# Running the recurrence's chunks of two head pairs kind by kind, with its gram products in quarters of the matmul array

## The chip, the cores and the metric

One core of one Trainium2 chip runs the whole program. The metric is device time in microseconds (us) of that core, the median of three runs. In the rows PE is the matmul engine (TensorE) and PEld its weight loads, DVE is VectorE, ACT is ScalarE, POOL is GpSimd, SP is the engine that issues most of the transfers, and L1612 is line 1612 of the kernel.

## What is computed

Two transformer blocks follow each other on 512 tokens of width 1024, all in float32. The first one has a gated linear recurrence, a convolution module, cross attention and feed-forward layers. The second one, in which the change lies, adds two mixers, a bidirectional RWKV-7 recurrence and a neighbourhood attention, and then a mixture of 32 experts. What matters here is the recurrence, with 8 heads of 64 channels and two directions d:

```python
def rwkv_step(S, inp):
    r_t, w_t, k_t, v_t, kk_t, a_t = inp
    sa = jnp.einsum('dbhij,dbhj->dbhi', S, -kk_t)
    S = (S * w_t[..., None, :] + sa[..., :, None] * (kk_t * a_t)[..., None, :]
         + v_t[..., :, None] * k_t[..., None, :])
    y = jnp.einsum('dbhij,dbhj->dbhi', S, r_t)
    return S, y
...
    S0 = jnp.zeros((2, B, RWKV_HEADS, HEAD_DIM, HEAD_DIM), jnp.float32)
    _, ys = lax.scan(rwkv_step, S0, xs)
    y_f = ys[:, 0].transpose(1, 0, 2, 3)
    y_b = jnp.flip(ys[:, 1].transpose(1, 0, 2, 3), axis=1)
    y = y_f + y_b
```

## The kernel before, in words

The kernel does not step token by token. It cuts the 512 tokens into 8 chunks of 64, and inside a chunk the steps become matrix products; only the 64x64 state passes from chunk to chunk. The 8 heads form 4 pairs p. One call `chunk(p, c)` does chunk c of both heads e of a pair and of both directions d: head 0 has partitions 0 to 63, head 1 has 64 to 127. There are 32 calls, with p running fastest.

What one call does, kind by kind, with the lines of the kernel before:

- L1577 and L1579 (in `fetch`, two calls ahead): two transfers of 64 KB (`w2`) and one of 192 KB (`bkv`), issued on SP. Each has three buffers.
- L1606: two transposes of the keys, copied by ACT to `bt` (L1607).
- L1612: the gram products, four matmuls of 64 rows by 128 columns. Each head has its own accumulator. A whole 128x128 product is made, of which one row half is masked into `w2` (L1615, DVE, 64x256) and a quarter into `rb` (L1617, DVE, 64x128). So DVE has four mask operations in each call.
- L1622: POOL scales the state by the decay into `ss`.
- L1626: four matmuls of the state with `w2` into `rh`, copied by DVE (L1629).
- L1633: four matmuls with the solved system `gt` into two accumulators, one for each head, copied into `su` by DVE and ACT (L1637).
- L1643: four matmuls for the state's update, with four DVE operations L1647 that write the next `su`.
- L1654 and L1658: eight matmuls for the output, added up in one accumulator `py` of both heads and added to the result by ACT or DVE (L1662 to L1666).

Each float32 matmul of these lines shows as two records in the trace. There are 5 accumulators of the kind `acc` and 3 of the kind `aux`.

Other work is put between the calls, as filler. It is the dense products (L524, L525, L526: three matmuls 128x512 for one block of a product in two-part float32), the neighbourhood attention (L1320 scores, L1350 transposes, L1357 values, and L635 and L1306), and the gates. Two strings of digits, `GATE` and `REST`, say how many steps of filler are released after each of the 32 calls. Within that, a scheduler sets the order of each engine's instructions when the program is built, so the code's order is not the engine's order: matmuls of neighbouring calls and of the filler are mixed, and each engine then runs its own list in order. After the last chunk of a head pair `finish` (L1676 onward) makes its normalised output.

Of the kernel before, what the change touches and what calls it, by code (L numbers as in the profile page):

```python
# [2 lines left out]

# [5 lines left out]
F32 = mybir.dt.float32  # L9
# [7 lines left out]
P = 128  # L17
S = 512
# [14 lines left out]
AHD = 2  # L33
# [178 lines left out]
HALF = (slice(0, 64), slice(64, P))  # L212
# [232 lines left out]
class Kernel:  # L445
# [689 lines left out]
    def final_norm(self):  # L1135


        nc = self.nc
        gf = self.v("final_norm", 0, DT)
        gg = self.C.tile([P, DT], F32, name="gg")  # L1140
        nc.vector.tensor_mul(gg, gf, self.v("norm1_g_2", 0, DT))
        xs = [self.split(t, scale=gg[:, i:i + 1]) for i, t in enumerate(self.x)]
        among = self.aheads(xs, "w_in_2", 0, range(8), (12, 13, 4, 0))
        for _ in range(6):
            next(among)
        r = self.rsqrt(self.by_token(*self.total(self.x, True, ends=ENDS)), 4, 1.0 / D)
# [10 lines left out]
        rb = self.M.tile([P, S], F32, name="rb", bufs=2)  # L1157
        nc.vector.tensor_copy(rb, self.spread(rr))
        rx = self.M.tile([P, S], F32, name="rb", bufs=2)
# [412 lines left out]

    def fetch(self, p, c):

        w2 = self.R.tile([P, 2, 2, P], F32, name="w2", bufs=AHD + 1)
        for e, a in enumerate(HALF):
            self.nc.sync.dma_start(w2[a, e], self.rec[p][c, a])  # L1577
        bkv = self.R.tile([P, 3, P], F32, name="bkv", bufs=AHD + 1)
        self.nc.sync.dma_start(bkv, self.bkv[p][c])  # L1579
        return w2, bkv  # L1580

    def chunk(self, p, c, w2, bkv):

        nc = self.nc
        R, M = self.R, self.M
# [2 lines left out]
        gt = self.gt[p // 2][:, n:n + 9:8]  # L1588


        own = lambda: R.tile([P, 2, 2, 2, 64], F32, name="su", bufs=5)
        if c == 0:
            self.su[p] = own()
            for e, a in enumerate(HALF):
# [7 lines left out]
        rb = R.tile([P, 2, 64], F32, name="rb", bufs=3)  # L1602
        bt = R.tile([P, 2, 2, 64], F32, name="bt", bufs=3)
        ps = self.acc()
        for d in range(2):
            nc.tensor.transpose(ps[:, d * P:(d + 1) * P], bk[:, d], self.idn)  # L1606
        nc.scalar.copy(bt.rearrange("p d e j -> p (d e j)"), ps[:, :2 * P])  # L1607
        for e in range(2):
            a, b = HALF[e], HALF[1 - e]
            ps = self.acc()  # L1610
            for d in range(2):
                nc.tensor.matmul(ps[:, d * P:(d + 1) * P], bk[a, d], w2[a, e, d], start=True,  # L1612
                                 stop=True)
            g = ps[:, :2 * P].rearrange("p (d t) -> p d t", d=2)
            nc.vector.tensor_mul(w2[b, e], g[b],  # L1615
                                 self.c("mk")[b, None, :].to_broadcast([64, 2, P]))
            nc.vector.tensor_mul(rb[a], g[a, :, 64:],  # L1617
                                 self.c("mi")[a, None, :].to_broadcast([64, 2, 64]))
        if c < 7:
            q = M.tile([P, 2, 64], F32, name="ss", bufs=4)  # L1620
            for e, a in enumerate(HALF):
                {'v': nc.vector, 'g': nc.gpsimd}[EB].tensor_mul(q[a], su[a, 0, e], el[a, :, c:c + 1].to_broadcast([64, 2, 64]))  # L1622
        pr = self.aux()
        for d in range(2):
            for e, a in enumerate(HALF):
# [1 line left out]
                                 start=True, stop=True)  # L1627
        rh = R.tile([P, 2, 64], F32, name="rh", bufs=2)
        nc.vector.tensor_copy(rh.rearrange("p d i -> p (d i)"), pr[:, :P])  # L1629
        pu = [self.aux(), self.aux()]  # L1630
        for d in range(2):
            for e, a in enumerate(HALF):
                nc.tensor.matmul(pu[e][a, d * 64:(d + 1) * 64], gt[a, d], rh[a, d],  # L1633
                                 start=True, stop=True)
        for e, a in enumerate(HALF):
            f = {'v': nc.vector.tensor_copy, 's': nc.scalar.copy}[EU[e]]
            f(su[a, 1, e].rearrange("p d i -> p (d i)"), pu[e][a, :P])  # L1637
        if c < 7:
            new = self.su[p] = own()
            pss = self.aux()  # L1640
            for d in range(2):
                for e, a in enumerate(HALF):
                    nc.tensor.matmul(pss[a, d * 64:(d + 1) * 64], bt[:, d, e], su[:, 1, e, d],  # L1643
                                     start=True, stop=True)
            for d in range(2):
                for e, a in enumerate(HALF):
                    nc.vector.scalar_tensor_tensor(new[a, 0, e, d], pss[a, d * 64:(d + 1) * 64],  # L1647
                                                   el[a, d, c:c + 1], q[a, d], op0=ALU.mult,
                                                   op1=ALU.add)
        py = self.aux()  # L1650

        for d in range(2):
            for e, a in enumerate(HALF):
                nc.tensor.matmul(py[a, d * 64:(d + 1) * 64], su[:, 0, e, d], w2[:, e, d, 64:],  # L1654
                                 start=d == 0, stop=False)
        for d in range(2):
            for e, a in enumerate(HALF):
                nc.tensor.matmul(py[a, d * 64:(d + 1) * 64], su[a, 1, e, d], rb[a, d], start=False,  # L1658
# [35 lines left out]
    def second_mixer(self):  # L1694
# [3 lines left out]
        with self.tc.tile_pool(name="systems", bufs=1) as G, \  # L1698
# [19 lines left out]
            self.Y, self.ya = self.x[:4], {}  # L1718
            with self.tc.tile_pool(name="chunks", bufs=1) as self.R:
                other, out = chain(near, gates), self.near_out()  # L1720
                gl = self.get("gl", self.R.tile([P, S], F32, name="gl"))
                ends = []
                slots = [(p, c) for c in range(8) for p in range(4)]
                recs = {n: self.fetch(*slots[n]) for n in range(AHD)}
                for n, (p, c) in enumerate(slots):
                    if n + AHD < len(slots):
                        recs[n + AHD] = self.fetch(*slots[n + AHD])
                    self.chunk(p, c, *recs.pop(n))
                    for g, at in ((gates, GATE), (other, REST)):
                        for _ in range(int(at[n])):  # L1730
                            next(g, None)
                    if c == 7:
                        if p == 0:
                            for _ in other:
                                pass
                        ends.append(self.finish(p, gl))
                        next(ends[p])
                        next(out)
                        if p > 1:
                            next(ends[p - 2])  # L1740
                            next(out)
                for e in ends[2:]:
                    next(e)
                    next(out)
# [420 lines left out]
```

## Time and profile before

| | us |
|---|---|
| runs | 2517.57, 2526.06, 2529.08 |
| median | 2526.06 |
| the profiled execution: its time | 2533.4 |
| the profiled execution: its span | 2531.6 |
| PE busy in the span | 2421.6 |
| the recurrence in the span | 1885 to 2127 |

The profiled execution is one run more, 7.3 us above the median. Its span runs from the first to the last instruction, and 1.8 us of its time lie around it. The last section before the prediction holds the rows of the trace on which the prediction rests. Times in them count from the span's start. A row of a timeline with "x8" merges eight records of one kind in a row, and its duration runs from the first one's start to the last one's end. The gap between the starts of neighbouring rows therefore says how long PE was taken by a row, and the duration does not, since matmuls overlap.

### The profile page before, as it was taken

The page shows a single profiled execution, that of the slowest core. Times are in us where ns is not written, and L with a number is a line of the kernel's source. Part 1 is how long each engine was busy: PE and PEld are TensorE (multiplying, and loading weights), DVE is VectorE, ACT ScalarE, POOL GpSimd, SP SyncE. Part 2 cuts the span into 40 slices and gives each one's busy share as a digit, 9 for nine tenths or more (in the row PEclk, how much of TensorE's full clock was granted, in tenths as well). Part 3 has the DMA queues.
Part 4 walks back from the last instruction along what each step waited for, and adds up shares of the span by engine and source line. Part 5 has one row for each costly group of instructions (what it writes and reads, how often), then busy time and mean ns, then how long its engine had stood idle before and what let it go on. Part 6 is the DMA issues. An engine that isn't in the chain of part 4 may idle for free.

```text
span 2531.6 us, 34476 instructions
## 1 busy us (share of the span) xinstructions
PE 2421.6 (96%) x13101; PEld 1863.7 (74%) x13101; DVE 1446.3 (57%) x2839; ACT 931.6 (37%) x1666; POOL 455.3 (18%) x428
## 2 busy tenths in 40 slices
PE   7999999999999999999999999898989999999996
PEld 6887888888887788888888887666777767764441
DVE  8988656444445456656445446788556776631110
ACT  4666444333333245444333334433233332321110
POOL 2112111110011000101110015343213320402211
PEclk9999999999999999999999999988879999989999
DMA  5332212222232213212322223445553344379998
GB/s 184 122 117 100 84 67 88 100 100 96 87 104 94 84 67 129 88 66 93 100 100 86 97 100 122 125 131 139 156 143 108 100 137 137 125 256 364 371 377 298
DMA packets 131195, 344.50 MB, mean 136 GB/s; under 512 B 40435, under 2 KB 66834, under 8 KB 101328
## 3 DMA queue, kind: packets, MB, share of 16 engines
q1 hardware_dynamic: 122944, 327.29, 37.9%
q0 software_dynamic: 5632, 10.49, 2.3%
q10 hardware_dynamic: 2448, 4.46, 0.5%
q8 instruction: 105, 1.72, 0.3%
q14 instruction: 66, 0.54, 0.1%
HBM read 307.33 MB, written 34.87 MB: 135 GB/s over the span
## 4 chain that ended last, share of the span: by engine, by line
PE 82%; DVE 10%; issue 2%; DMA 2%; ACT 2%; POOL 1%; SPq 0%; POOLq 0%; DVEq 0%; ACTq 0%
PE acc L524 20%; PE acc L525 20%; PE acc L526 20%; PE acc L2011 4%; PE aux L1995 3%; PE acc L2038 2%; DVE wlo L356 1%; PE acc L1612 1%; DMA raw<-wex 1%; PE aux L635 1%; DVE z L1529 1%; PE aux L592 1%; PE aux L1320 1%; DVE rs L615 1%; PE aux L1633 1%
## 5 line engine op out<-in xcount | busy, mean ns | idle before, releaser
L353 ACT CAST whi<-raw 128x512 fp32r<-128x512 f32 x652 | 398.6, 620 | 765.6 <-PE acc L525 641.2
L524 PE MATMUL acc<-xn,whi 128*128 128x512 f32 x1656 | 662.9, 401 | 12.6 <-ACT xn L562 6.6
L526 PE MATMUL acc<-xn,wlo 128*128 128x512 f32 x1656 | 658.3, 398 | 3.8 <-DVE wlo L356 3.8
L525 PE MATMUL acc<-xn,whi 128*128 128x512 f32 x1656 | 660.2, 399 | 0.0
L356 DVE TENSOR_TENSOR wlo<-raw,whi 128x512 fp32r<-128x512 f32 x605 | 446.4, 743 | 304.8 <-ACT whi L353 302.8
L524 PEld LDWEIGHTS acc<-xn,whi 128*128 128x128 f32 x1656 | 317.2, 192 | 84.4 <-ACT xn L562 6.6
L526 PEld LDWEIGHTS acc<-xn,wlo 128*128 128x128 f32 x1656 | 317.1, 192 | 72.6 <-DVE wlo L356 4.7
L525 PEld LDWEIGHTS acc<-xn,whi 128*128 128x128 f32 x1656 | 317.4, 192 | 72.0 <-issue 6.2
L524 PE MATMUL acc<-act,whi 128*128 128x512 f32 (+1 forms) x676 | 254.1, 377 | 3.1 <-DVE tmp L1761 1.8
L525 PE MATMUL acc<-act,whi 128*128 128x512 f32 (+1 forms) x676 | 254.0, 376 | 2.2 <-DVE act L560 2.2
L526 PE MATMUL acc<-act,wlo 128*128 128x512 f32 (+1 forms) x676 | 253.9, 376 | 0.0
L698 POOL TENSOR_TENSOR tmp<-tmp 128x512 f32<-128x512 f32 x48 | 74.3, 1549 | 628.0 <-DVE tmp L696 560.9
L582 POOL TENSOR_TENSOR tmp<-tmp 128x512 f32<-128x512 f32 x56 | 80.5, 1437 | 422.5 <-ACT tmp L575 404.0
L524 PEld LDWEIGHTS acc<-act,whi 128*128 128x128 f32 x676 | 128.1, 190 | 28.9 <-DVE tmp L1761 2.3
L525 PEld LDWEIGHTS acc<-act,whi 128*128 128x128 f32 x676 | 128.1, 190 | 27.6 <-DVE act L560 2.6
L526 PEld LDWEIGHTS acc<-act,wlo 128*128 128x128 f32 x676 | 128.1, 190 | 25.1
L560 DVE TENSOR_TENSOR act<-tmp,act 128x512 fp32r<-128x512 f32 x88 | 61.1, 695 | 87.1 <-ACT act L559 85.1
L559 ACT CAST act<-tmp 128x512 fp32r<-128x512 f32 x88 | 54.4, 620 | 122.2 <-POOL tmp L698 91.2
L2043 POOL DMA_INDIRECT out<-tmp,tid x32 | 50.7, 1583 | 246.3 <-ACT tmp L2042 156.5
L356 POOL TENSOR_TENSOR wlo<-raw,whi 128x512 fp32r<-128x512 f32 x47 | 63.8, 1360 | 138.8 <-ACT whi L353 119.9
L678 DVE SCALAR_TENSOR_TENSOR tmp<-tmp,vec 128x512 f32<-128x512 f32 x96 | 72.1, 752 | 17.1 <-ACT tmp L675 15.3
L2011 PE MATMUL acc<-raw,xn 128*64 128x512 f32 x320 | 75.8, 602 | 4.5 <-DMA raw<-wex 4.4
(425 smaller groups left out, 3364.4 us busy)
## 6 DMA issues: line engine op xcount, KB each, us to landing
raw<-wst SPq DMA_DIRECT2D x162, 1024.0 KB, 5.0
raw<-wex SPq DMA_DIRECT2D x56, 1024.0 KB, 16.0
whi<-wex SPq DMA_DIRECT2D x56, 256.0 KB, 7.1
wlo<-wex SPq DMA_DIRECT2D x56, 256.0 KB, 6.0
x<-wex SPq DMA_DIRECT2D x12, 1024.0 KB, 9.8
bkv<-bkv SPq DMA_DIRECT2D x32, 192.0 KB, 2.5
rec<-ab SPq DMA_DIRECT2D x8, 512.0 KB, 3.8
sp_gate<-tmp ACTq DMA_DIRECT2D x16, 256.0 KB, 2.1
```

What stands on the lines that cost most here:

```text
L353: self.nc.scalar.copy(hi, raw)
L356: rest.tensor_sub(lo, raw, hi.bitcast(F32))
L524: nc.tensor.matmul(ps, w[0], x[0], start=first, stop=False)
L525: nc.tensor.matmul(ps, w[0], x[1], start=False, stop=False)
L526: nc.tensor.matmul(ps, w[1], x[0], start=False, stop=last)
L559: nc.scalar.copy(h, src)
L560: nc.vector.tensor_sub(lo, src, h.bitcast(F32))
L582: nc.gpsimd.tensor_add(n, accs.pop(), t)
L678: nc.vector.scalar_tensor_tensor(z, h[:, k:k + S], taps[k], y, op0=ALU.mult, op1=ALU.add)
L698: nc.gpsimd.tensor_mul(z, u, ge)
L1995: nc.tensor.matmul(ps[:, k * 256:(k + 1) * 256], x[:, j * P:(j + 1) * P], self.at[g][j // 2][:, j % 2], start=n + j == 0, stop=n * 4 + j == 7)
L2011: nc.tensor.matmul(pg[a], h[:, o:o + SLOTS], w[2 * k + n], start=c + k == 0, stop=c + k == 4)
```

## The change

- `chunk` becomes a generator that stops between its kinds of product. After each odd call the chunks of two head pairs (p = 0 and 1, or 2 and 3) are run together: kind by kind, first of the one, then of the other.
- The gram products are made in quarters of the array. Four matmuls of 64 rows by 128 columns whose result lies in the other head's partitions go to one accumulator `ps` (L1614), and four of 64 by 64 to a second accumulator `po` (L1618). Both accumulators now hold both heads. What is left out is the quarter of the product that nobody read. The mask into `rb` becomes one DVE operation of 128x128 (L1624) in place of two.
- L1642 (before L1633) writes both heads into one accumulator.
- `w2`, `bkv`, `rb` and `bt` get a fourth buffer and a `w2` or `bkv` is fetched as before two calls ahead; `su` gets a sixth, `ss` gives one up. `gl` moves into another pool's buffer.
- `finish` is called for two pairs at once, after the last chunk of the odd one.

```diff
-        w2 = self.R.tile([P, 2, 2, P], F32, name="w2", bufs=AHD + 1)
+        w2 = self.R.tile([P, 2, 2, P], F32, name="w2", bufs=AHD + 2)
...
-        bkv = self.R.tile([P, 3, P], F32, name="bkv", bufs=AHD + 1)
+        bkv = self.R.tile([P, 3, P], F32, name="bkv", bufs=AHD + 2)
...
         nc.scalar.copy(bt.rearrange("p d e j -> p (d e j)"), ps[:, :2 * P])
+        yield
+
+        ps, po = self.acc(), self.acc()
+        for d in range(2):
+            for e in range(2):
+                a, b = HALF[e], HALF[1 - e]
+                nc.tensor.matmul(ps[b, d * P:(d + 1) * P], bk[a, d, b], w2[a, e, d], start=True,
+                                 stop=True)
+        for d in range(2):
+            for e, a in enumerate(HALF):
+                nc.tensor.matmul(po[a, d * 64:(d + 1) * 64], bk[a, d, a], w2[a, e, d, 64:],
+                                 start=True, stop=True)
         for e in range(2):
-            a, b = HALF[e], HALF[1 - e]
-            ps = self.acc()
-            for d in range(2):
-                nc.tensor.matmul(ps[:, d * P:(d + 1) * P], bk[a, d], w2[a, e, d], start=True,
-                                 stop=True)
-            g = ps[:, :2 * P].rearrange("p (d t) -> p d t", d=2)
-            nc.vector.tensor_mul(w2[b, e], g[b],
+            b = HALF[1 - e]
+            nc.vector.tensor_mul(w2[b, e], ps[b, :2 * P].rearrange("p (d t) -> p d t", d=2),
                                  self.c("mk")[b, None, :].to_broadcast([64, 2, P]))
-            nc.vector.tensor_mul(rb[a], g[a, :, 64:],
-                                 self.c("mi")[a, None, :].to_broadcast([64, 2, 64]))
+        nc.vector.tensor_mul(rb, po[:, :P].rearrange("p (d t) -> p d t", d=2),
+                             self.c("mi")[:, None, :].to_broadcast([P, 2, 64]))
...
-        pu = [self.aux(), self.aux()]
+        yield
+        pu = self.aux()
...
-                nc.tensor.matmul(pu[e][a, d * 64:(d + 1) * 64], gt[a, d], rh[a, d],
+                nc.tensor.matmul(pu[a, d * 64:(d + 1) * 64], gt[a, d], rh[a, d],
...
-                    self.chunk(p, c, *recs.pop(n))
+                    if n % 2:
+                        two = [self.chunk(*slots[i], *recs.pop(i)) for i in (n - 1, n)]
+                        for _ in zip_longest(*two):
+                            pass
```

The scheduler puts this into an engine order of its own. On PE, in the middle of the recurrence, this stood before, from the L1626 of one call (its `w2` is w_16891) to that of the next call:

```order
L1626 MATMUL aux<-su,w_16891 64x64 x4
L524 MATMUL acc<-xn,whi 128x512
L525 MATMUL acc<-xn,whi 128x512
L526 MATMUL acc<-xn,wlo 128x512
L1633 MATMUL aux<-rh,gt_12736 64x64 x4
L524 MATMUL acc<-xn,whi 128x512
L525 MATMUL acc<-xn,whi 128x512
L1643 MATMUL aux<-su,bt 64x64 x4
L1654 MATMUL aux<-w_16891,su 64x64 x4
L1658 MATMUL aux<-rb,su 64x64 x4
L1320 MATMUL aux<-ab 128x256 x2
L1626 MATMUL aux<-su,w_16996 64x64 x4
```

At the same place of the changed program PE has this (L1634 is the old L1626, L1642 the old L1633, L1653 the old L1643, L1665 and L1670 the old L1654 and L1658; w_16832 and w_16850 are the `w2` of the two calls):

```order
L1634 MATMUL aux<-su,w_16832 64x64 x4
L1634 MATMUL aux<-su,w_16850 64x64 x4
L526 MATMUL acc<-xn,wlo 128x512
L1642 MATMUL aux<-rh,gt_12736 64x64 x8
L524 MATMUL acc<-xn,whi 128x512
L1653 MATMUL aux<-su,bt 64x64
L525 MATMUL acc<-xn,whi 128x512
L1653 MATMUL aux<-su,bt 64x64 x7
L1665 MATMUL aux<-w_16832,su 64x64 x4
L1670 MATMUL aux<-rb,su 64x64 x4
L526 MATMUL acc<-xn,wlo 128x512
L524 MATMUL acc<-xn,whi 128x512
```

The kinds of two calls now stand together (L1634 twice, L1642 and L1653 with eight), and one row of filler parts two kinds where two or three parted them.

Near the recurrence's end, where little filler is left, PE had this before, right behind the last L1654 of a call whose `w2` is w_18155:

```order
L1658 MATMUL aux<-rb,su 64x64 x4
L1626 MATMUL aux<-su,w_18251 64x64 x4
L1612 MATMUL acc<-w_18313,bkv 128x128 x4
L1606 MATMUL acc<-cst,bkv 128x128 x2
L1633 MATMUL aux<-rh,gt_12735 64x64 x4
L1643 MATMUL aux<-su,bt 64x64
L1654 MATMUL aux<-w_18251,su 64x64 x3
L1643 MATMUL aux<-su,bt 64x64 x3
L1654 MATMUL aux<-w_18251,su 64x64
L1658 MATMUL aux<-rb,su 64x64 x4
L1626 MATMUL aux<-su,w_18313 64x64 x4
L1612 MATMUL acc<-w_18375,bkv 128x128 x3
```

There PE has this in the changed program:

```order
L1665 MATMUL aux<-w_17902,su 64x64 x4
L1670 MATMUL aux<-rb,su 64x64 x4
L1665 MATMUL aux<-w_17937,su 64x64 x4
L1670 MATMUL aux<-rb,su 64x64 x4
L1349 MATMUL aux<-cst,tmp 128x128 x4
L1614 MATMUL acc<-w_18295,bkv 64x128
L1618 MATMUL acc<-w_18295,bkv 64x64
L1356 MATMUL aux<-tmp,ab 64x128 x4
L1634 MATMUL aux<-su,w_18103 64x64 x4
```

With three buffers, w_18375 took the buffer of w_18155, which is free ahead of the first of the rows before, and its gram product (L1612, the last row) stands a whole call later. With four buffers w_18295 takes that of w_17902, which the first row of the changed piece frees, and its gram product (L1614) stands behind four more rows.

## Rows read from the trace of the kernel before

**Rows 1.** The page: busy time and share of PE; chain that ended last.

```profile
PE 2421.6 (96%) x13101; PEld 1863.7 (74%) x13101; DVE 1446.3 (57%) x2839; ACT 931.6 (37%) x1666; POOL 455.3 (18%) x428
PE 82%; DVE 10%; issue 2%; DMA 2%; ACT 2%; POOL 1%; SPq 0%; POOLq 0%; DVEq 0%; ACTq 0%
```

**Rows 2.** Windows of the recurrence: us, busy (x), then PEclk, DMA share, GB/s.

```profile
1945.00:1975.00 30.00, 29.88 (x303) 21.20 (x303) 24.49 (x74) 11.62 (x37) 8.69 (x19) 1.00 0.49 155
2005.00:2035.00 30.00, 29.91 (x307) 21.32 (x306) 23.86 (x77) 11.15 (x33) 8.94 (x20) 1.00 0.24 72
2065.00:2095.00 30.00, 26.80 (x306) 20.55 (x308) 20.77 (x72) 4.68 (x14) 7.04 (x18) 0.73 0.47 154
```

**Rows 3.** Timeline of PE, 2008.4 to 2012.6: start, us, line, operation.

```profile
2008.53 0.50 PE L524 MATMUL acc<-xn,whi 128*128 128x512 f32 x1
2008.86 0.39 PE L525 MATMUL acc<-xn,whi 128*128 128x512 f32 x1
2009.09 0.39 PE L526 MATMUL acc<-xn,wlo 128*128 128x512 f32 x1
...
2011.39 0.38 PE L1606 MATMUL acc<-cst,bkv 128*128 128x128 f32 x2
2011.70 0.72 PE L1612 MATMUL acc<-w,bkv 64*128 64x128 f32 x8
```

**Rows 4.** Timeline of PE, 2013.8 to 2016.4.

```profile
2014.24 0.45 PE L1633 MATMUL aux<-rh,gt 64*64 64x64 f32 x8
2014.62 0.50 PE L526 MATMUL acc<-xn,wlo 128*128 128x512 f32 x1
2014.96 0.40 PE L524 MATMUL acc<-xn,whi 128*128 128x512 f32 x1
2015.28 0.45 PE L1643 MATMUL aux<-su,bt 128*64 128x64 f32 x8
2015.57 0.40 PE L1654 MATMUL aux<-w,su 128*64 128x64 f32 x8
2015.90 0.45 PE L1658 MATMUL aux<-rb,su 64*64 64x64 f32 x8
2016.28 0.48 PE L1320 MATMUL aux<-ab 64*128 64x256 f32 x1
```

**Rows 5.** Timeline of PE at 2019: gram products of one head alone.

```profile
2019.05 0.71 PE L1612 MATMUL acc<-w,bkv 64*128 64x128 f32 x4
```

**Rows 6.** Line L1612, its matmuls; line L1617, its DVE operations: ns min/median/max.

```profile
L1612 PE MATMUL acc<-w,bkv x256: 269/272/579, 1886.1 to 2122.1; 64*128 64x128 f32 x128
L1617 DVE TENSOR_TENSOR rb<-acc,cst x64: 271/288/295, 1887.8 to 2122.8; 64x128 f32<-64x128 f32 x64
```

**Rows 7.** Waits of PE, 1880 to 2127: waited for, us in total, times, longest.

```profile
PE acc L1606 <- issue: 4.8, 1, 4.8
PE aux L635 <- DVE rs L617: 3.6, 2, 1.9
PE acc L1612 <- DMA w<-rec: 1.8, 1, 1.8
PE aux L1626 <- DVE w L1615: 1.3, 3, 0.6
```

**Rows 8.** Windows at the recurrence's end, columns as in the rows 2.

```profile
2065.00:2078.00 13.00, 10.44 (x156) 7.93 (x156) 11.48 (x40) 2.79 (x8) 3.88 (x10) 1.00 0.71 247
2080.00:2099.00 19.00, 19.00 (x160) 14.26 (x156) 11.09 (x38) 1.90 (x6) 3.16 (x8) 0.50 0.19 55
```

**Rows 9.** Timeline of SP, 2064 to 2080: transfers issued.

```profile
2071.20 0.42 SPq L430 DMA_DIRECT2D raw<-wex  x1
2072.30 4.85 SPq L1577 DMA_DIRECT2D w<-rec  x4
```

**Rows 10.** Line L1577: its transfers, from issue to landing.

```profile
DMA to landing us min/median/max: 2.0/2.3/6.3
```

**Rows 11.** Windows behind the recurrence, columns as in the rows 2.

```profile
2247.00:2257.00 10.00, 9.01 (x57) 9.04 (x58) 6.50 (x26) 1.36 (x4) 0.00 (x0) 0.69 0.12 48
2277.00:2287.00 10.00, 10.00 (x62) 5.53 (x58) 1.65 (x3) 1.65 (x3) 3.29 (x2) 1.00 1.02 352
```

More of the change, by code (lines that the diff above doesn't have):

```diff
@@ L1 @@
 from contextlib import ExitStack
-from itertools import chain, islice
+from itertools import chain, zip_longest
 import numpy as np
@@ L1156, in final_norm @@
             pass
-        rb = self.M.tile([P, S], F32, name="rb", bufs=2)
+        rx, rb = (self.M.tile([P, S], F32, name="rb", bufs=2) for _ in range(2))
         nc.vector.tensor_copy(rb, self.spread(rr))
-        rx = self.M.tile([P, S], F32, name="rb", bufs=2)
         nc.vector.tensor_copy(rx, self.spread(r))
@@ L1588, in chunk @@
         gt = self.gt[p // 2][:, n:n + 9:8]
-        own = lambda: R.tile([P, 2, 2, 2, 64], F32, name="su", bufs=5)
+        own = lambda: R.tile([P, 2, 2, 2, 64], F32, name="su", bufs=6)
         if c == 0:
@@ L1601, in chunk @@
             f(su[b, :, e], v[b].to_broadcast([64, 2, 2, 64]))
-        rb = R.tile([P, 2, 64], F32, name="rb", bufs=3)
-        bt = R.tile([P, 2, 2, 64], F32, name="bt", bufs=3)
+        rb = R.tile([P, 2, 64], F32, name="rb", bufs=4)
+        bt = R.tile([P, 2, 2, 64], F32, name="bt", bufs=4)
         ps = self.acc()
@@ L1607, in chunk @@
         nc.scalar.copy(bt.rearrange("p d e j -> p (d e j)"), ps[:, :2 * P])
[L1608 to L1615 removed]
+        yield
[9 more added lines that the diff above has]
+                                 start=True, stop=True)
+        for e in range(2):
+            b = HALF[1 - e]
+            nc.vector.tensor_mul(w2[b, e], ps[b, :2 * P].rearrange("p (d t) -> p d t", d=2),
                                  self.c("mk")[b, None, :].to_broadcast([64, 2, P]))
[L1617 to L1618 removed]
+        nc.vector.tensor_mul(rb, po[:, :P].rearrange("p (d t) -> p d t", d=2),
+                             self.c("mi")[:, None, :].to_broadcast([P, 2, 64]))
         if c < 7:
[L1620 removed]
+            q = M.tile([P, 2, 64], F32, name="ss", bufs=3)
             for e, a in enumerate(HALF):
                 {'v': nc.vector, 'g': nc.gpsimd}[EB].tensor_mul(q[a], su[a, 0, e], el[a, :, c:c + 1].to_broadcast([64, 2, 64]))
+        yield
         pr = self.aux()
@@ L1636, in chunk @@
             f = {'v': nc.vector.tensor_copy, 's': nc.scalar.copy}[EU[e]]
-            f(su[a, 1, e].rearrange("p d i -> p (d i)"), pu[e][a, :P])
+            f(su[a, 1, e].rearrange("p d i -> p (d i)"), pu[a, :P])
+        yield
         if c < 7:
@@ L1649, in chunk @@
                                                    op1=ALU.add)
+        yield
         py = self.aux()
@@ L1655, in chunk @@
                                  start=d == 0, stop=False)
+        yield
         for d in range(2):
@@ L1720, in second_mixer @@
                 other, out = chain(near, gates), self.near_out()
-                gl = self.get("gl", self.R.tile([P, S], F32, name="gl"))
+                gl = self.get("gl", self.M.tile([P, S], F32, name="rb", bufs=2))
                 ends = []
@@ L1731, in second_mixer @@
                             next(g, None)
-                    if c == 7:
-                        if p == 0:
+                    if c == 7 and p % 2:
+                        if p == 1:
                             for _ in other:
                                 pass
[L1736 to L1740, printed above, removed]
+                        for i in (p - 1, p):
+                            ends.append(self.finish(i, gl))
+                            next(ends[i])
                             next(out)
+                            if p > 1:
+                                next(ends[i - 2])
+                                next(out)
                 for e in ends[2:]:
```

1 line of the change is left out of this document (added).

## The prediction

> **What bounds the kernel now.** I read first the page's busy times and its chain that ended last. PE is busy for 96% of the span and holds 82% of the chain [rows 1], so the time is PE's own list of instructions. The recurrence takes 242 us of it, 1885 to 2127. Second came the windows of that stretch. In its body PE is busy for 29.9 of 30 us at a granted clock of 1.00, and DVE for 24 of 30 [rows 2]. Towards its end PE has 26.8 of 30 at 0.73. So there are two places with different limits: a body in which only PE's stream counts, and an end, with little filler, in which waits and the clock count.
>
> Third came the timeline of PE, for the price of the stream. In a row of equal matmuls the dense ones start 0.23 us apart (2008.86 to 2009.09 [rows 3]). Where the shape of the tile (128*128, 128*64, 64*64) changes, the starts lie further apart. L1643 to L1654, both 128*64, are 0.29 apart, of which 0.05 is the entry of L1643 (its eight records take 0.45, those of L1654 0.40). So eight records of 64 columns take 0.24, a pitch of 0.06 for each two that run side by side. L1654 to L1658, where the shape changes, is 0.33 [rows 4]: leaving a shape costs 0.09. The first dense matmul after a change is 0.34 from the second (2014.62 to 2014.96), not 0.23: entering costs 0.11 there. **One switch of shape** therefore costs 0.09 + 0.05 = 0.14 us into shapes of 64 columns and 0.09 + 0.11 = 0.20 into those of 128.
>
> Fourth, the gram products. The eight records of both heads take 0.72 us, and the four of one head alone 0.71 [rows 3, 5]: the row halves of the array run side by side. One record lasts 0.27 [rows 6] and two transposes 0.38 [rows 3], so the pitch at 128 columns is 0.11.
>
> Last, the waits of PE: 4.8 us for the first fetch, 3.6 at L635, 1.8 for one `w2`, 1.3 for a mask [rows 7], and half a clock from 2080 to 2099, with PE busy all the time [rows 8].
>
> **The change part by part.**
>
> *Switches of shape.* Counted in PE's order from the first L1606 to the program's end, switches into shapes with 128 columns go from 293 to 232, and into shapes with 64 columns from 269 to 290, since the dense blocks are now cut into smaller pieces between the kinds. That is -61 x 0.20 + 21 x 0.14 = -12.2 + 2.9 = **-9.3 us**. The stream is PE's own, nothing hides it, so all of it counts.
>
> *Gram products.* Before, a call whose two heads stand together costs 4 pitches x 0.11 = 0.44, and one whose heads are parted 0.88. The order has 60 pieces for 32 calls, and their sum is 22.0 us. After, a call has four pairs of pitch 0.11 and four of pitch 0.06. Its quarters are all of the array's four: the 64-column ones use the two that the 128-column ones leave free. If four can run at once, 0.44 and a rest of 0.08 are left, 16.7 us with the pieces as they stand. If only two run at once it is 0.72 a call, 23.1 us. So the bounds are -5.3 and +1.1. The trace shows row halves side by side [rows 3, 5] and column halves (L1654), not four quarters, but the four lie in different places of the array, as the halves do, so I take **-5.3**.
>
> *One accumulator for both heads* (L1642, L1614, L1618). L1633 writes two accumulators before and L1658 one. Both are 0.38 from the next row (2014.24 to 2014.62, 2015.90 to 2016.28 [rows 4]). I count 0. The Trainium skill, page "TensorEngine Tiling (Array Packing)", section "Gotcha 1: PSUM Pressure", says that "different row tiles cannot access same PSUM bank simultaneously"; the row of L1658 speaks against it, and what it would give is the last rival.
>
> *DVE.* One mask L1624 takes the place of two of 0.288 us [rows 6], 32 x 0.288 = 9.2 us less. In the body DVE is not what PE waits for, so it counts 0; the cover is PE's stream, and if DVE were the bound the gain would be those 9.2 us. At the end of the recurrence it can take something off the 1.3 us at L1626 [rows 7].
>
> *The first wait.* The first fetch no longer stands behind that of `gl` on SP, and four attention matmuls now stand in the 4.8 us [rows 7]. L635 may wait one time more. Bounds -1.3 and +2; I take **-1**.
>
> *The fetch at the end.* A `w2` lands 2.3 us after its issue, at worst 6.3 [rows 10]. Before, a gram product stands a whole call, some 3.5 to 4.5 us, behind the product that frees its buffer; it waited once, 1.8 us, when a 1 MB transfer had gone out 1.1 us ahead [rows 9]. After, the next pair's gram products stand behind L1670, L1665, L1670 and four attention matmuls: about 3 x 0.33 [rows 4], and 4 x 0.11 with a switch of 0.20, 1.6 us in all. Three or four pairs stand so. Where nothing else is in the queue the wait is 2.3 - 1.6, with the second issue on SP some 1 to 2 us; two of them stand behind a `raw<-wex` on SP too, as the one that waited. What is queued behind the waiting matmul is the whole of PE. I take 1 + 2 + 3 = 6 us in place of 1.8, **+4.2**. Bounds 0 (at half clock the lead doubles) and +12.
>
> *Copies, state, finish.* The eight operations L1647 of two calls follow each other on DVE, 2 x 1.2 us, under the products of the other pair; `finish` of an even pair comes one call later. I count 0, with +-2 for both.
>
> *What comes behind.* The experts' weights saturate the transfers from 2277 on (share 1.02), but from 2247 to 2257 they rest (0.12) because all buffers are full [rows 11]. So what is gained ahead is not lost there.
>
> **Sum:** -9.3 - 5.3 - 1 + 4.2 = **-11.4 us**. The profiled run, 2533.4, would become 2522.0. It lies 7.3 above the median of 2526.06, so the median becomes 2514.7, said as 2515. The stretches at half clock move this by some 3 us: what the stream loses there counts twice.
>
> **Rivals.**
>
> *Only two tiles at a time.* The gram term is +1.1 and the sum -5: 2521. For it: no row shows four at a time. Against it: the halves, in both directions, cost nothing beside each other.
>
> *The clock at the end holds.* The half clock of 2080 to 2099 [rows 8] came after a stretch in which PE was busy for 10.4 of 13 us. If the two calls side by side fill that stretch, the 19 us become 9.5, and the time is about 2505. Against it are the waits for `w2` that I expect at the same place.
>
> *The fetch decides.* If the pairs at the end wait for 6.3 - 1.6 = 4.7 us twice and 1.5 twice, that is 12.4 us instead of 6, and if these waits bring another 20 us at half clock it costs 10 more. The sum is -11.4 + 6.4 + 10 = +5: 2531. It turns into a loss as soon as the waits at the end and the lost clock take more than 15.6 us, what the stream and the first wait give.
>
> *One accumulator in turns.* Were matmuls of two row halves into one accumulator to take turns, L1642 would cost 0.24 more a call, and the gram products 8 x 0.11 + 8 x 0.06 = 1.36 instead of 0.69. With 32 calls that is 7.7 + 21.4 - 9.3 + 3.2 = +23: 2549, slower. Against it stands L1658 [rows 4], for it no row. By the page's rule above the time would be this one.
>
> **How the numbers follow.** The forecast has 0.47 (its own range 2507 to 2523), two at a time 0.22, the clock that holds 0.14, the fetch 0.13, turns 0.04. The range of 2501 to 2533 leaves out the turns, the far ends of the fetch and of the clock, and the runs' own spread (2517.6 to 2529.1). Measurement can tell about 0.5% from no change, 12.6 us: faster is below 2513.4, slower above 2538.7. Faster: the clock and somewhat under half of the forecast, 0.38. Slower: turns and the far end of the fetch, 0.09. The rest, 0.53, is within 0.5%.
>
> **What would show it.** In the changed profile, the timeline of the body should show L1614 and L1618 of one call ending within some 0.6 us of starts; 0.75 or more says two at a time. L1642's eight records should take 0.45 and be 0.38 from the next row; 0.6 says turns. The waits of PE should show the `w<-rec` transfers with about 6 us, at the last pairs; 12 or more says that the fetch decides. The window of the last 30 us of the recurrence should have a clock near 0.73; 1.00 says that the clock held. The recurrence, from the first L1606 to the last L1670, should be about 230 us. If it is not under 238, a step of the sum is wrong. If it is 230 and the time has not moved, the loss is behind it.

## The result and the profile after

The changed kernel takes 2505.65 us in the median (2500.62 to 2523.07), the kernel before in the same comparison 2526.32. The ratio is 0.9919, with a 95% interval of 0.9902 to 0.9936. That is 20.7 us faster, where 11.4 had been forecast.

The page of the changed kernel, in the columns of [rows 1], still shows PE as the engine that the time goes by:

```profile
PE 2389.0 (96%) x13357; PEld 1841.1 (74%) x13357; DVE 1430.8 (57%) x2807; ACT 928.3 (37%) x1666; POOL 454.1 (18%) x428
...
PE 78%; DVE 10%; DMA 4%; issue 4%; ACT 2%; POOL 1%; SPq 0%; POOLq 0%; DVEq 0%; ACTq 0%
```

The two profiled executions lie 31 us apart, more than the medians. Both kernels run nearly the same instructions up to the first L1606, which starts at 1885.5 us before and at 1876.4 after. A second profile of the kernel before (below) had it at 1880.5 and one of the changed kernel at 1877.6. So most of those 9 us are the two executions' own luck with the clock ahead of the recurrence. The comparison that counts starts at the first L1606 and ends at the first transposes for the router (L1853 before, L1869 after), by when the same work has been done but for a few attention matmuls. It leaves out the wait in front of the first L1606. These are windows over that stretch; behind the length stands the busy time of PE, and the granted clock is the third number from the end. The kernel before, in its first profile and in the second:

```profile
1885.50:2195.50 310.00, 298.31 (x2480) 219.63 (x2481) 212.15 (x624) 98.27 (x247) 81.33 (x148) 0.94 0.37 119
```

```profile
1880.50:2190.70 310.20, 297.84 (x2480) 219.37 (x2481) 212.59 (x624) 98.25 (x247) 81.08 (x148) 0.94 0.38 118
```

The changed kernel, in its first profile and in the second:

```profile
1876.40:2167.40 291.00, 275.19 (x2723) 202.32 (x2724) 196.25 (x591) 94.52 (x246) 78.37 (x144) 0.97 0.41 127
```

```profile
1877.60:2170.60 293.00, 275.52 (x2724) 202.79 (x2725) 197.25 (x591) 94.42 (x246) 78.45 (x144) 0.97 0.40 126
```

The stretch is 17 to 19 us shorter, in both pairs. What is not busy is PE's waiting. A part of the busy time in stretches at a clock of 0.50 is what the clock took, and the rest is the stream at full clock. The first guess for that part is one half, and the expectations below count so. It is too much. Two profiles of one and the same program, the kernel with the quarters alone (below), ran the same stretch at the end of the recurrence, once at full and once at half clock; the columns are those of [rows 2]:

```profile
2048.58:2067.40 18.82, 16.50 (x290) 12.09 (x290) 14.07 (x50) 3.15 (x10) 6.65 (x17) 1.00 0.53 162
2048.81:2075.73 26.92, 26.45 (x290) 19.57 (x290) 15.11 (x54) 3.15 (x10) 6.62 (x17) 0.50 0.39 116
```

PE is busy for 26.45 us in place of 16.50, so the clock took 0.38 of the busy time, and the stretch is 8.1 us longer. This price of 0.38 is an estimate from one stretch of small matmuls. It is borne out by the profiles taken again: with it the stream of one, or nearly one, order of instructions comes out the same whatever its clock (283.3 twice before and 283.0 with four buffers; 275.3, 275.1 and 275.2 with the quarters alone), and with one half it doesn't (278.6, 278.7 and 276.8; 273.9, 270.1 and 270.2).

| from the first L1606 to the router | length | PE waits | lost, at one half | stream, at one half | lost, at 0.38 | stream, at 0.38 |
|---|---|---|---|---|---|---|
| before | 310.0 | 11.7 | 19.7 | 278.6 | 14.9 | 283.3 |
| before, second profile | 310.2 | 12.4 | 19.1 | 278.7 | 14.5 | 283.3 |
| after | 291.0 | 15.8 | 7.9 | 267.3 | 6.0 | 269.2 |
| after, second profile | 293.0 | 17.5 | 8.8 | 266.8 | 6.7 | 268.9 |

So the stream gives some 14 us, the clock 8 to 9, and PE waits 4 to 5 us more within the stretch. Counted at one half it would be 11 to 12 and 10 to 12.

**The stream.** This is the timeline of PE in the body of the recurrence, after:

```profile
1991.71 0.60 PE L1606 MATMUL acc<-cst,bkv 128*128 128x128 f32 x4
1992.24 0.65 PE L1614 MATMUL acc<-w,bkv 64*64 64x128 f32 x8
1992.82 0.50 PE L524 MATMUL acc<-xn,whi 128*128 128x512 f32 x1
...
1993.96 0.27 PE L1618 MATMUL acc<-w,bkv 64*64 64x64 f32 x2
1993.99 0.33 PE L1614 MATMUL acc<-w,bkv 64*64 64x128 f32 x2
1994.07 0.28 PE L1618 MATMUL acc<-w,bkv 64*64 64x64 f32 x4
1994.15 0.28 PE L1614 MATMUL acc<-w,bkv 64*64 64x128 f32 x2
1994.19 0.22 PE L1618 MATMUL acc<-w,bkv 64*64 64x64 f32 x2
1994.26 0.39 PE L1614 MATMUL acc<-w,bkv 64*64 64x128 f32 x4
1994.58 0.67 PE L1356 MATMUL aux<-tmp,ab 128*64 128x128 f32 x8
```

The L1618 records start inside the L1614 records, 0.03 us behind each other (1993.96 and 1993.99). These are the L1618 of one call and the L1614 of the other. Sixteen records take 0.62 us from the first start to L1356. The eight of L1614 alone take 0.58 to the next row (1992.24 to 1992.82). So all four quarters of the array run at once, and the 64-column quarters are nearly free. The row of L1642 says the same of one accumulator for two row halves; these are both calls' sixteen records:

```profile
2037.41 0.68 PE L1642 MATMUL aux<-rh,gt 64*64 64x64 f32 x16 [0.35 <-DVE rh L1637]
```

Eight pairs in 0.68 us, of which the last record lasts 0.22, are a pitch of 0.066, that of matmuls side by side. Nothing takes turns.

**The clock.** In the kernel before there are four stretches at half clock within the recurrence, nearly the same in both profiles: 12.6 us at its start, two of 3.4 us, and 20.5 us at its end. The last one, in the columns of [rows 2]:

```profile
2079.00:2099.50 20.50, 20.50 (x178) 15.45 (x176) 11.79 (x40) 2.15 (x7) 3.16 (x8) 0.50 0.23 67
```

After, there are these three:

```profile
1876.40:1883.00 6.60, 5.76 (x49) 3.82 (x49) 2.28 (x7) 0.74 (x2) 2.08 (x6) 0.50 0.78 229
1910.20:1913.60 3.40, 3.40 (x20) 2.50 (x22) 1.69 (x9) 1.27 (x4) 0.00 (x0) 0.51 0.04 8
2053.60:2060.40 6.80, 6.57 (x81) 5.33 (x80) 3.04 (x10) 0.79 (x3) 1.20 (x4) 0.50 0.52 183
```

The one at the end is 6.8 us long, and 10.2 in the second profile. The one at the start ends 6.6 us into the recurrence instead of 12.6. Four attention matmuls now stand in the first wait, and the kernel with interleaved calls and the old gram products has the same shorter stretch; that these matmuls are the reason was not tested. At 0.38 the end gives 4 to 5 of the 8 to 9 us, the start 2.4 and the short stretch that is gone 1.3.

**The waits,** from the first L1606 to the router, to be read against [rows 7]:

```profile
PE aux L635 <- DVE rs L617: 3.0, 4, 1.4
PE acc L1614 <- DMA w<-rec: 2.9, 2, 2.7
PE acc L1606 <- DMA bkv<-bkv: 2.1, 2, 1.3
PE acc L524 <- DVE tmp L1777: 1.8, 1, 1.8
PE aux L1634 <- DVE w L1622: 1.6, 3, 0.7
```

The wait for `w2` at the end is there, once and 2.7 us long (2049.6 to 2052.3), where three or four with 6 us in all had been forecast. A handful of short ones behind copies fills up the rest. The wait in front of the first L1606, 4.8 us before [rows 7], is 1.3 us after, with 0.7 at the attention matmuls (L1356) that now stand in it. With these, PE waits 16.5 and 17.2 us before and 17.8 and 19.5 after, 1.3 and 2.3 more.

### The profile page after: what moved, and what is told of

The parts are those of the page before. It is cut to its first block, busy times and chain, and to the rows that moved or that the text cites. A ratio compares the mean times of both kernels' runs of the same rounds, so it can differ in the third digit from the quotient of the medians.

```text
span 2500.4 us, 34970 instructions
## 1 busy us (share of the span) xinstructions
PE 2389.0 (96%) x13357; PEld 1841.1 (74%) x13357; DVE 1430.8 (57%) x2807; ACT 928.3 (37%) x1666; POOL 454.1 (18%) x428
## 4 chain that ended last, share of the span: by engine, by line
PE 78%; DVE 10%; DMA 4%; issue 4%; ACT 2%; POOL 1%; SPq 0%; POOLq 0%; DVEq 0%; ACTq 0%
PE acc L524 20%; PE acc L525 20%; PE acc L526 20%; PE acc L2027 3%; PE aux L2011 2%; DMA raw<-wex 2%; PE acc L2054 1%; DVE wlo L356 1%; DMA wlo<-wex 1%; PE aux L592 1%; PE aux L1319 1%; PE aux L1653 0%; PE aux L1566 0%; DVE rs L615 0%; PE aux L1634 0%
## 5 line engine op out<-in xcount | busy, mean ns | idle before, releaser
L524 PE MATMUL acc<-xn,whi 128*128 128x512 f32 x1656 | 661.1, 400 | 13.2 <-ACT xn L562 6.9
L526 PE MATMUL acc<-xn,wlo 128*128 128x512 f32 x1656 | 657.3, 397 | 3.8 <-DVE wlo L356 3.8
L524 PEld LDWEIGHTS acc<-xn,whi 128*128 128x128 f32 x1656 | 315.5, 191 | 84.0 <-ACT xn L562 6.9
L526 PEld LDWEIGHTS acc<-xn,wlo 128*128 128x128 f32 x1656 | 315.7, 191 | 71.6 <-DVE wlo L356 4.7
L524 PE MATMUL acc<-act,whi 128*128 128x512 f32 (+1 forms) x676 | 255.3, 378 | 3.1 <-DVE tmp L1777 1.8
L526 PE MATMUL acc<-act,wlo 128*128 128x512 f32 (+1 forms) x676 | 254.7, 377 | 0.0
L524 PEld LDWEIGHTS acc<-act,whi 128*128 128x128 f32 x676 | 129.5, 192 | 28.8 <-DVE tmp L1777 2.2
L526 PEld LDWEIGHTS acc<-act,wlo 128*128 128x128 f32 x676 | 129.3, 191 | 24.9
L2027 PE MATMUL acc<-raw,xn 128*64 128x512 f32 x320 | 75.8, 602 | 4.5 <-DMA raw<-wex 4.4
```

The lines of the kernel that those rows point to most:

```text
L524: nc.tensor.matmul(ps, w[0], x[0], start=first, stop=False)
L526: nc.tensor.matmul(ps, w[1], x[0], start=False, stop=last)
L2027: nc.tensor.matmul(pg[a], h[:, o:o + SLOTS], w[2 * k + n], start=c + k == 0, stop=c + k == 4)
```

## The experiments

The theory at this point was that the stream gives what the count of switches and gram pieces says, and that the other half of the gain is the half clock at the recurrence's end. The open questions were which part of the change gives the stream, and what the half clock hangs on: the wait for `w2`, the stretch without dense products, the interleaving, or chance. For the timed runs a second split helps: span times mean granted clock ("at full clock", waits included) and the remainder ("lost"), as means over all timed runs of a kernel. This "lost" is half of all the time at half clock, from the start of the program, so it is more than the clock took. Each ratio is to the kernel before in the same comparison.

| kernel | ratio to before | interval | at full clock, us | lost, us |
|---|---|---|---|---|
| before (29 runs) | 1 | | 2447 | 75 |
| after | 0.9919 | 0.9902 to 0.9936 | 2438 | 66 |
| quarters alone | 0.9958 | 0.9943 to 0.9973 | 2437 | 73 |
| interleaving alone | 0.9970 | 0.9957 to 0.9983 | 2444 | 72 |
| before, four buffers | 0.9986 | 0.9973 to 0.9999 | 2441 | 78 |
| before, filler spread | 0.9978 | 0.9963 to 0.9992 | 2451 | 66 |
| after, filler spread | 0.9923 | 0.9900 to 0.9947 | 2440 | 63 |
| quarters, filler spread | 0.9943 | 0.9925 to 0.9961 | 2445 | 65 |
| after, pairs not interleaved | 1.0056 | 1.0035 to 1.0076 | 2449 | 88 |
| after, filler ahead of pairs | 0.9903 | 0.9871 to 0.9935 | 2434 | 66 |

The lost time of a single run lies up to 8 to 18 us off its kernel's mean, so a single profile can mislead by that much.

### Quarters alone, the calls one after another

The kernel before with this of the change:

```diff
         for e in range(2):
-            a, b = HALF[e], HALF[1 - e]
-            ps = self.acc()
-            for d in range(2):
-                nc.tensor.matmul(ps[:, d * P:(d + 1) * P], bk[a, d], w2[a, e, d], start=True,
-                                 stop=True)
...
+        ps, po = self.acc(), self.acc()
...
+        nc.vector.tensor_mul(rb, po[:, :P].rearrange("p (d t) -> p d t", d=2),
+                             self.c("mi")[:, None, :].to_broadcast([P, 2, 64]))
```

> The kernel before with the gram products and masks of the changed one, the calls one after another. In PE's order the switches of shape go from 293 + 269 to 239 + 317 (into 128 and into 64 columns), -54 x 0.20 + 48 x 0.14 = -4.1 us; the gram pieces from 22.2 to 15.4 us, -6.8. If the stream alone counts: -10.9 us, ratio 0.9957, and the half clock at the recurrence's end stays (some 20 us at 0.50). If the clock at the end holds here too: another -10, ratio 0.992, and the interleaving has no share in the gain.

The ratio came out at 0.9958, that of the stream alone (0.9957). The first profile had no half clock at the end at all, but it was also the fastest of 12 runs. Two more profiles were taken of the same kernel:

> The kernel with the quarters alone, for a second profile. The first one was its fastest run (2502 against a median of 2513) and had no half clock at the recurrence's end. If the clock there varies from run to run, this one has 10 to 20 us at 0.50 near the end and a time near 2513; the stream from the first L1606 to the first L1848 stays at 274 us, 4.7 less than before.

> The kernel with the quarters alone, a third profile for its clock at the end: none in the first, 27.3 us at 0.50 in the second. If it varies from run to run, either may come.

Both (2513.11 and 2512.50 us) had 27.3 us at half clock near the end, with PE busy for 26.5 of them:

```profile
2048.50:2075.80 27.30, 26.52 (x290) 19.64 (x291) 15.42 (x56) 3.15 (x10) 6.87 (x18) 0.50 0.39 116
```

The stream at 0.38 was 275.3, 275.1 and 275.2 us in the three, so the quarters bring it down by 8 us, where 10.9 had been expected. They do nothing lasting for the clock (73 us lost over the runs, against 75), and the first profile would have told the opposite.

### Interleaving alone, with the gram products of before

The changed kernel with the loop over `e`, its two accumulators and four masks put back. It keeps all else of the change: the fourth buffers, the late `finish`, the one accumulator of L1642. What is called interleaving here is all of that together.

> The changed kernel with the gram products and four masks of before; the calls of two pairs stay interleaved. Switches 263 + 260, so -30 x 0.20 - 9 x 0.14 = -7.3 us; gram pieces 18.9 us, -3.3. By the stream: -10.6 with +2 to +4 for waits on w2 at the end, ratio 0.997. If the interleaving is what keeps the clock up at the end, another -10: ratio 0.993, and the last 30 us of the recurrence have a granted clock of 0.9 or more.

0.9970, as the stream with its waits said. From the first L1606 to the router: 303.9 us, of which waits 17.0 and, at 0.38, lost to half clock 11.1 and stream 275.8. So the interleaving takes 7.5 us off the stream, gives 5 back in waits, and there were 17.1 us of half clock at the end. It doesn't hold the clock by itself. The two parts alone give 0.9958 x 0.9970 = 0.9928, and together 0.9919. The first lies within the interval of the second, so the times alone don't show that the two parts help each other.

### Four buffers in the kernel before

```diff
-        w2 = self.R.tile([P, 2, 2, P], F32, name="w2", bufs=AHD + 1)
+        w2 = self.R.tile([P, 2, 2, P], F32, name="w2", bufs=AHD + 2)
...
-        bkv = self.R.tile([P, 3, P], F32, name="bkv", bufs=AHD + 1)
+        bkv = self.R.tile([P, 3, P], F32, name="bkv", bufs=AHD + 2)
```

> The kernel before with four buffers of w2 and bkv in place of three, else the same (the fetch still goes out two calls ahead). The stream does not change (298 + 269 switches). If the 1.8 us wait for w2 at 2077 brought on the half clock of 2079 to 2099, both are gone: -12 us, ratio 0.995. If the half clock comes from how little PE has to do there, only the wait goes: ratio 0.999, with some 20 us at 0.50 near the end.

The wait for `w2` is gone from the waits of PE, and the half clock at the end is longer, 37.5 us, although PE was busy for 36.4 of them:

```profile
2054.80:2092.30 37.50, 36.39 (x307) 27.36 (x308) 20.73 (x75) 3.79 (x12) 6.25 (x16) 0.50 0.35 109
```

So the wait doesn't bring on the half clock. The Trainium skill, page "TensorE: Matmul & The Clock Gate", section "HAM oscillation — how this bites in real kernels", puts such losses on gaps in which PE is idle. This case's trace does not agree: the gap was taken away, and the half clock of the one profile was longer, 37.5 us in place of 20.5. Over the runs 78 us were lost, against 75, so all that they show is that it didn't go away.

### The kernel before, again

> The kernel before, unchanged, for a second profile. If the half clock at the recurrence's end belongs to this order of instructions, it is there again, some 17 to 24 us long, behind a wait for w2. If it is chance, it is missing or half as long. The half clock ahead of the recurrence (1613 to 1885) lost 40 us of time in the first profile and 26 in that of the changed kernel: by chance the second profile lies anywhere between.

20.5 us at half clock at the end, from 2073.5 to 2094.0, as in the first profile to the tenth of a microsecond, and, counted at one half, 26 us lost between 1613 us and the recurrence in place of 40, as in the changed kernel. So the half clock at the end came again with this order of instructions. What is lost ahead of it varies.

### The changed kernel, again

> The changed kernel, unchanged, for a second profile. If its shorter half clock belongs to its order of instructions, PE loses 4 to 12 us to the half clock between the first L1606 and the first L1869, as the 7.9 of the first profile, and not the 19 to 20 of both profiles of before. If that was chance, it lies nearer to 20. The stream there should be 267 us again, with waits of some 16.

8.8 us lost and stream 266.8, counted at one half as the expectation does, and waits 17.5. So the shorter half clock came again too. Two profiles are few, with 0, 27.3 and 27.3 us in the three of the quarters alone; the means over the timed runs (66 us lost, against 75 before, 73 with the quarters and 72 with the interleaving) say the same.

### The same filler, spread over the calls

In the kernel before the steps of filler are used up by the 22nd call, and no dense product runs from 2061.1 to 2096.5. Only the two strings change:

```diff
-GATE = "01111111011110110111111101210110"
-REST = "11211212112112121111121311111212"
+GATE = "01011010110110101011010110101100"
+REST = "01111111110111111111011111111100"
```

> The kernel before with the same steps of filler spread over 30 calls in place of the first 22 (only the two strings GATE and REST change), so that dense products stand between nearly all calls. The stream hardly changes (296 + 269 switches). If the half clock at the end comes from the 35 us without dense products, some 20 us at 0.50 go and with them the waits there: -10 to -13 us, ratio 0.9955. If it comes from elsewhere, or if the calls early in the recurrence now lack cover, the ratio is 1.000 or above.

0.9978, half of what had been expected. The half clock at the end is gone. A window near the end of the recurrence, of the kernel before:

```profile
2061.10:2096.50 35.40, 31.85 (x343) 24.32 (x341) 25.91 (x88) 6.87 (x18) 7.83 (x20) 0.75 0.47 147
```

And of this one:

```profile
2066.00:2114.00 48.00, 47.89 (x399) 32.43 (x397) 33.30 (x97) 17.72 (x40) 5.44 (x7) 1.00 0.48 164
```

In the profile the stretch from the first L1606 to the router is 304.8 us, 5.2 less than before. At 0.38 the clock gives 6.6 of that, the stream is unchanged (283.2), as expected, and PE waits 1.5 us more. The expectation had priced 20 us of half clock at 10, where 0.38 makes 7.8 of it. So dense products at the end do keep the clock: in none of the four kernels with spread filler (this one and the three below) is there half clock at the end.

The same strings in the changed kernel:

> The changed kernel with the same steps of filler spread over 30 calls. Switches 295 + 243 in place of 290 + 232: +11 x 0.20 + 5 x 0.14 = +2.9 us; gram pieces 14.9 in place of 17.0, -2.1. If the end without dense products is what costs the changed kernel its waits (2.7 us for w2 at 2049.6, some 4 us for copies) and 4 us of clock, these go: -6 to -8 us against the changed kernel, ratio 0.989 to before. If nothing at the end is to be had, 0.992 as the changed kernel.

0.9923, no better than the changed kernel. The half clock at the end is gone here too, but in the changed kernel there was little left to be had: at 0.38, 6.0 became 3.5 us lost, and the stream took 1.4 of that back (269.2 became 270.6).

And in the kernel with the quarters alone:

> The quarters alone with the steps of filler spread over 30 calls, the calls one after another: no interleaving. If the stream gain is the quarters' and the clock gain is to be had by dense products at the end, their sum is the whole gain without the interleaving: -8 of stream and -9 of clock with +3 of switches and waits, ratio 0.9935 to 0.995. If the interleaving is needed for more than that, 0.996 or above.

0.9943, inside what was expected: the clock as after (65 us lost), the stream not (278.5 us at 0.38, 3.3 more than with the quarters alone, the +3 that had been expected).

### Two calls released together, but not interleaved

```diff
-                        for _ in zip_longest(*two):
+                        for _ in chain(*two):
```

> The changed kernel with one word changed: the two calls of a pair are released together as before, with the quarters, the buffers and the late finish, but one call after the other and not kind by kind. Switches 331 + 236, so 62 x 0.14 - 57 x 0.20 = -2.7 us against the kernel before; gram pieces 17.9, -4.3; with the quarters' measured surplus some -8. If the interleaving is what shortens the half clock at the end, it is 15 us or longer here and the ratio is 0.996, as with the quarters alone. If releasing two calls together is enough, the half clock there is under 11 us and the ratio is 0.992 to 0.993.

Neither: the half clock at the end is 13.7 us, between the two conditions, and the time is 2540.65 us, 1.0056, slower than the kernel before and 35 us slower than the changed kernel. Waits of PE from the first L1606 to the router:

```profile
PE aux L635 <- DVE rs L617: 6.3, 4, 3.0
PE aux L1642 <- DVE rh L1637: 5.9, 8, 1.1
PE aux L1653 <- ACT su L1646: 3.8, 9, 0.6
```

They are 24.0 us in all in place of 15.8; at 0.38 the stream is 279.7 in place of 269.2, and 15.6 us are lost to half clock in place of 6.0. So the waits make 8 of the 28 us by which the stretch is longer, the stream over 10 and the clock over 9. L1642 waits eight times for the copy of its operand, and L1653 nine times for the copy of L1642's result. The filler is released behind both calls, so what stood between the products of a call is missing, and only the other call's products can fill the time of those copies. The forecast had counted this cover as nothing, because PE's own stream would do it. One word of the change is worth 1.4% here.

### Filler in front of the pairs

The changed kernel, with the steps released ahead of each pair and over 28 calls:

```diff
-GATE = "01111111011110110111111101210110"
-REST = "11211212112112121111121311111212"
+GATE = "10101020101020101010201010200000"
+REST = "10202020202020202020202020200000"
```

> The changed kernel with the same steps of filler released in front of each pair, spread over 28 calls (the two strings alone). Switches 275 + 222 in place of 290 + 232, -15 x 0.14 - 10 x 0.20 = -4.1 us; gram pieces 15.7 in place of 17.0, -1.3. If the stream price holds and the end keeps its clock as in the first spread (3 us less lost): -5 to -8 us against the changed kernel, ratio to before 0.989. If the switches are over-priced, as the changed kernel suggests (it gained 11.3 of 14.6), half of that, and if the dense products taken from the early pairs leave waits there, 0.992 or above.

0.9903 and a median of 2500.84, 4.8 us under that of the changed kernel. The intervals overlap, so that it is faster than the changed kernel isn't settled; it is faster than the kernel before. From the first attention scores (L1319) to the router it takes 346.2 us, against 350.1 and 353.0 in the two profiles of the changed kernel, and no half clock is left in the recurrence but that at its start.

## Why the prediction was right, and where it was not

**The bound** was read rightly: PE's list, and two places with different limits.

**Switches and gram products** (-9.3 and -5.3, -14.6 in all): 14.1 and 14.4 us were measured, at 0.38 for the half clock, and about 1 of that is attention that went ahead of the first L1606. Four quarters at once was right. (For the rival of two at a time, four pitches of 0.11 and four of 0.06 add up to 0.68 a call and 21.8 us, not to 0.72 and 23.1; it would have been 2520.) Taken by line, from one start to the next without waits and at full clock, the stream moved as follows in the first two profiles:

| lines, before / after | before, us | after, us |
|---|---|---|
| gram products, L1612 / L1614, L1618 | 34.6 | 23.2 |
| dense products, L524 to L526 | 132.2 | 134.2 |
| attention, L1306, L1320, L1350, L1357 / one line less | 27.5 | 23.5 |
| L1606 | 11.0 | 10.0 |
| L1626 / L1634 | 13.5 | 13.6 |
| L1633 / L1642 | 12.2 | 10.3 |
| L1643 / L1653 | 7.9 | 10.2 |
| L1654 / L1665 | 11.8 | 12.9 |
| L1658 / L1670 | 12.6 | 12.1 |
| all other lines | 20.0 | 19.2 |

Most of the gain, 11.4, is in the gram products and the switches at their edges. The dense blocks, cut into smaller pieces, cost 2.0 more. L1643 and L1654 stood in one row of a single shape before and are parted in places after, 3.4 more. The attention gains 4.0, with the 1 that only moved. So the step was right, in its kind and, within 1 to 2 us, in its size. That each single switch has the price read at two places is not shown: with the quarters alone 8 us came of 10.9, and with the interleaving alone 7.5 of 10.6.

**One accumulator for both heads** (0): right, by the row of L1642 and the four quarters. The last rival is excluded.

**The waits** (-1 and +4.2, +3.2 together): +1.3 and +2.3 with the wait in front of the first L1606, so the sum was 1 to 2 us too high, and its make-up was off. The first wait gave 2 us in place of 1. The fetch was mis-sized: 6 us in place of 1.8 were expected and 2.9 and 2.7 came, in place of 1.8 and 2.4. It cost 2.7 us once in each profile. The `raw<-wex` that was to lengthen it was issued at 2043.6, 3.1 us ahead of the fetch, and not 1.1 as before. Short waits for copies, which had been put at nothing, made up the rest.

**The clock** (0, with 3 us either way): here the sum failed. It gave 8 to 9 us in the recurrence. The rival "the clock at the end holds", with -10 and a chance of 0.14, had a part of it: 4 to 5 us came at the end, the rest at the start and in a short stretch, of which the prediction says nothing. The rival was argued from waits that the two calls would fill, and these turned out not to be the cause: the waits for `w2` were even longer than before, PE was busy for 28.98 of the 35.5 us without dense products where it had been for 31.85 of 35.4, and yet the clock was at half for 6.8 and 10.2 us in place of 20.5. Its price, one half of the time at half clock, was too high; that what the stream loses there "counts twice" was too much for the same reason. What the runs show is that dense products at the end keep the clock, with either kernel; that the wait for `w2` doesn't drive it; and that neither part of the change alone shortens the half clock reliably (27.3 us twice and none once with the quarters, 17.1 us with the interleaving), while both together did so in both profiles. Why a stretch of 35.5 us without dense products loses its clock for only 7 to 10 us in the changed kernel, and one of 49 us for 13.7 us with its pairs not interleaved, is not settled. So what the changed order does to the clock is measured and not explained.

**The cover of copies** (0): right for the change, but only because of the interleaving, as the run without it shows.

**What comes behind** (nothing lost there): right. From the router to the first product with an expert's weights (L2011 before, L2027 after) it is 63.4 us in both profiles before and 62.2 and 63.4 after, and from there to the end 272.7 and 270.2 before and 270.8 and 273.5 after.

**The signs.** Two of them could not tell what they were meant to. The recurrence, from the first L1606 to the last L1670, fell from 241.1 to 210.6 and 212.8 us, not to 230, but 26 of its 261 dense products and other filler now stand behind it. And its last 30 us had a clock of 0.95 before already; nearly all of the half clock lies ahead of them.

In all, the sum of -11.4 had the stream about right, the waits 1 to 2 us too high, and lacked the 8 to 9 us of the clock, nearly all of the difference to the measured 20.7. That 2505.65 lies in the range of 2501 to 2533 is in part luck: it lies outside the forecast's own range of 2507 to 2523, and near the 2505 of the rival that had the clock in it, whose reason did not hold. "Faster" had a chance of 0.38.

## What to carry to other kernels

Count PE's stream by start-to-start times and by shape switches; where small products use two quarters of the array and leave two free, put a third and fourth product there. Work that is taken out of one kind of product shows up as cuts in its neighbours, so add up all lines of the stretch and not only the ones that were edited. When two dependent chains are released together, run them step by step against each other: one behind the other they wait for their own copies. And give the clock a term of its own in the sum wherever a stretch is left without dense work. Price it from one stretch that ran at either level, not as one half; one profile isn't enough to size it.

## What the runs showed of the hardware

Four quarter tiles, two with 128 and two with 64 columns, ran at once: sixteen records in 0.62 us, where eight took 0.58. Two row halves wrote one accumulator side by side (a pitch of 0.066 us).

The granted clock stayed at 0.50 for up to 37.5 us while PE was busy nearly all the time (36.4 us). For the first 31 of them it ran 64-row and 64-column tiles and transposes, and no dense products. In six profiles it went up again 2 to 10 us after the first dense product, and in three ahead of it (the changed kernel twice, and the one with its pairs not interleaved). Removing a wait ahead of the fall did not prevent it. The same small matmuls kept PE busy for 26.45 us at half clock and for 16.50 at full clock, a factor of 1.6 and not 2.
